# Decoder block on one core: buffers of the mixer's output product and of the cross attention moved to pools of their own

## The chip, the cores and the metric

The kernel runs on one core of a Trainium2 chip (8 cores in two dies; seven of them are idle here). A core has five engines that run their own instruction queues side by side: TensorE (PE, with its weight loads shown as PEld), VectorE (DVE), ScalarE (ACT), GpSimd (POOL) and SyncE (SP, which here only starts transfers). They share an on-chip memory (SBUF, 128 partitions) and 16 DMA engines that move data from and to the main memory. The metric is the device time of one execution in microseconds (us). Differences of under about 0.5% can't be told from no change with this kernel.

## The reference

One decoder layer on `x` (512 tokens x 1024), 256 memory tokens, all in float32:

```
def reference(x, mem, ...):
    x = x + hybrid_mixer(rmsnorm(x, norm_mix_w[l]), ...)           # ends with  mixed @ w_out
    x = x + memory_cross_attention(rmsnorm(x, norm_xa_w[l]), rmsnorm(mem, norm_mem_w[l]), xa_wq, xa_wkv, xa_wo)
    x = x + peer_ffn(rmsnorm(x, norm_ffn_w[l]), ...)               # 8 heads x 16 of 16384 experts per token
    return rmsnorm(x, norm_final_w)

def memory_cross_attention(h, m, wq, wkv, wo):
    q = (h @ wq).reshape(b, s, XA_HEADS, XA_HEAD_DIM)
    k, v = jnp.split(m @ wkv, 2, axis=-1)
    scores = einsum('bshd,bmhd->bhsm', q, k) * XA_HEAD_DIM ** -0.5
    return einsum('bhsm,bmhd->bshd', softmax(scores), v).reshape(b, s, D_MODEL) @ wo
```

`hybrid_mixer` holds two recurrences (gated DeltaNet and mLSTM, four heads each); their outputs, side by side, are `mixed`. `peer_ffn` fetches for every token 128 rows of `u_table` and 128 rows of `v_table`.

## The kernel before

The 512 tokens are four tiles of 128. The work runs in stages: the mixer (with the keys and values of the memory worked in), the mixer's output product, cross attention, the routing of the expert layer, and the expert layer itself, which fetches rows for tiles 0 and 1 with indirect transfers on POOL's queue while tiles 2 and 3 are done densely over the whole tables. A scheduler puts the instructions of each engine in order when the program is built. It also gives every buffer its place: buffers belong to pools, a pool is opened on the left or the right side of the SBUF, and the memory of a closed pool can be given to another one, whose instructions then wait for the instructions that used what lay there.

Three pieces of code meet at the place that changes.

- `mixer` (line 598) opens the pools `mxp` and `mxw` and holds them until its last line. Among the buffers of `mxp` is `hT`, 32 KB a partition. It holds the normed input, transposed and split in a high and a low half, and, under the same name, later `mixed` in the same form (lines 687 to 689).
- The mixer's output product is `residual(..., "wout")` (lines 691 to 692): for tiles 0 and 1, then for tiles 2 and 3, 8 weight blocks of 512 KB each. For a block, SP loads it into one of two buffers `w` (line 246), ACT writes its high half `wh` (236), DVE the low half `wl` (223), and PE does 12 matmuls (271). DVE adds the finished sums to `X` (700). Only when DVE has made the low half may SP load the next but one block.
- `xattn` (704) begins behind it. Its buffers `W0`, `W1`, `W2`, `dh0` and `dh1` are all in the pool `late`, on the right side, over the place of `mxp` and `mxw`. `wr` (the weight row of the norm) is loaded into `W1` by POOL (709, 191). `norm` (724) takes a tile's squares on ACT (197), works out one over the root in 12 small DVE operations (174 to 183), scales on DVE (199), transposes on PE (209) and writes the high half on ACT (211) and the low one on DVE (212) into `dh0` (tiles 0 and 1, called `G0`) or `dh1` (tiles 2 and 3, `G1`). `query` (728) multiplies by `wq`: 8 blocks of 24 matmuls (284) for `G0`, with weights split by ACT (251) into `W2`, their low halves made in turn by POOL (221) and DVE (223).

`ORDER_XA` (line 56) lists the order in which the cross attention and what follows are written: `w2 n0 q008 n1 s0 x0 ...` (weights' buffers, norm of `G0`, its queries in 8 blocks, norm of `G1`, ...).

Of the kernel before, what the change touches and what calls it, by code (L numbers as in the profile page):

```python
# [6 lines left out]
F32 = mybir.dt.float32  # L7
F32R = mybir.dt.float32r
# [8 lines left out]
P = 128  # L17
D = 1024
DB = D // P
# [50 lines left out]
def hymba_kernel(tc, A, out, dbg=None):  # L70
    from contextlib import ExitStack
    with ExitStack() as ctx:
        _body(ctx, tc, A, out, dbg or {})


def _body(ctx, tc, A, out, dbg):
    from contextlib import ExitStack
    nc = tc.nc
    V, SC, PE, G = nc.vector, nc.scalar, nc.tensor, nc.gpsimd

    def pool(name, bufs=1, **kw):
        return ctx.enter_context(tc.tile_pool(name=name, bufs=bufs, **kw))
# [15 lines left out]
    def tap(name, ap):  # L98
        if name in dbg:
            nc.sync.dma_start(dbg[name], ap)  # L100
# [64 lines left out]
    X = {}  # L165
# [36 lines left out]
    def transposed(src, hs, i):  # L202

        ts = slice(i * P, (i + 1) * P)
        for g in range(2):
            ps = psT.tile([P, 4, P], F32, name="tr")
            for b in range(4):
                c = (4 * g + b) * P
                PE.transpose(ps[:, b], src[:, c:c + P], I)
            d = slice(4 * g, 4 * g + 4)  # L210
            SC.activation(hs["h"][:, d, ts], ps, AF.Copy)
            V.tensor_tensor(hs["l"][:, d, ts], ps, hs["h"][:, d, ts], op=OP.subtract)

    def hbuf(ph, n, name="hT"):
        t = ph.tile([P, 2, DB, n * P], F32R, name=name, bufs=1)
        return {"h": t[:, 0], "l": t[:, 1]}
# [9 lines left out]
    low_on, count, spare = [V, G, G], [0], []  # L226
# [31 lines left out]
    def proj(hs, n, w, blocks, evac):  # L258

        for nb in blocks:  # L260
            acc = [psA.tile([P, 512], F32, name="pj") for _ in range(n)]
            for kc in range(4):
                if "f" in hs:
                    pairs = [(hs["f"], unsplit(w[nb, kc], 2))]
                else:
                    pairs = passes((hs["h"], hs["l"]), weights(w[nb, kc]))
                for i in range(n):
                    for z in range(2):
                        d = kc * 2 + z
                        for m, (a, b) in enumerate(pairs):  # L270
                            PE.matmul(acc[i], a[:, d, i * P:(i + 1) * P], b[:, z], start=d == 0 and m == 0,  # L271
                                      stop=d == DB - 1 and m == len(pairs) - 1)
            for i in range(n):
                evac(nb, i, acc[i])
# [53 lines left out]
    def run(steps, n=1000):  # L328
        for _ in range(n):
            if next(steps, steps) is steps:  # L330
                break
# [265 lines left out]

    def mixer(tiles, aside):
        nt = len(tiles)
        with tc.tile_pool(name="mxp", bufs=nt) as ph, tc.tile_pool(name="mxw", bufs=2) as wk:  # L600
            ph = Phase(ph, tiles)
            hs = hbuf(ph, nt)
            mixed = {}
            steps = aside(wk)
            wr = wpool.tile([P, D], F32, name="wh")
# [78 lines left out]
            nc.sync.dma_start(x, A["x"].rearrange("(a p) d -> p a d", p=P))  # L684
            for ti in range(NT):
                X[ti] = x[:, ti]
            hs = hbuf(ph, nt)
            for i, ti in enumerate(tiles):
                transposed(mixed[ti].rearrange("p a b -> p (a b)"), hs, i)
            low_on[:] = [V]  # L690
            for k in range(0, nt, 2):
                residual(tiles[k:k + 2], {z: t[:, :, k * P:(k + 2) * P] for z, t in hs.items()}, "wout")
            for ti in tiles:
                tap(f"x1_{ti}", X[ti])

    def residual(tiles, hs, w):
        def ev(nb, i, ps):
            x = X[tiles[i]]
            c = slice(nb * 512, nb * 512 + 512)
            V.tensor_tensor(x[:, c], ps, x[:, c], op=OP.add)  # L700
        proj(hs, len(tiles), A[w], range(2), ev)
# [365 lines left out]
    def peer_gather(ready, buffer):  # L1067
# [51 lines left out]
        G.dma_start(*close(G0[1]))  # L1119

    mixer(tuple(range(NT)), memory_kv)
    mxs.close()
    late = pool("late", 1, side="right")
# [5 lines left out]
    dh = []  # L1129

    def eight(t):
        return t[:, 0:2].rearrange("p a b -> p (a b)").rearrange("p (a b) -> p a b", a=DB)
    for i in range(2):
        t = late.tile([P, 2, DB, 2 * P], F32R, name=f"dh{i}")
        dh.append({"h": t[:, 0], "l": t[:, 1]})
    pe = ctx.enter_context(ExitStack())
    sct = pe.enter_context(tc.tile_pool(name="sct", bufs=1, side="right"))
# [7 lines left out]
    def row_numbers():  # L1145
        for a in range(K):
            for x, val in enumerate((start[a], start[a] - start[a - 1] if a else 0, a)):
                tc.keep_in_program_order(G.memset(rows_[:, x, a], float(val)))
    pew = pe.enter_context(tc.tile_pool(name="pew", bufs=2, side="right"))

    def opened(g):
        g.open(pe.enter_context(tc.tile_pool(name="pep", bufs=g.nt, side="right")))
        return g
# [15 lines left out]
    def settle(group, ti):  # L1169
        group.finish(ti, slot)  # L1170
        t0 = DENSE.index(ti) * P
        for t in range(t0, t0 + P, TG):
            stages.append(stages.pop(0))
            build(t, bufs, stages[-1], bank4)
            yield

    def ahead(n):
        for _ in range(n):
            ps = psA.tile([P, 512], F32, name="pj")[:, :T]
            times(unsplit(A["pt"][count_a[0]]), second.h, ps)  # L1180
            act_(count_a[0], ps)
            count_a[0] += 1

    def blocks(t):
        return t.rearrange("p a b -> p (a b)").rearrange("p (e t) -> p e t", t=T)
# [9 lines left out]
    for what in ORDER_XA.split():  # L1195
        kind, n = what[0], int(what[1:])
        if kind == "n":
            norm(GS[n])
        elif kind == "q":
            n, x, y = (int(c) for c in what[1:])  # L1200
            query(GS[n], range(x, y))
            if n and y == DB:
                t = late.tile([P, 4, D], F32, name="dh1")
                dh[1] = {"f": eight(t), "room": t}
        elif kind == "s":
            soft_[n] = soft(n)
        elif kind == "x":
            mix(n, *soft_[n])
        elif kind == "o":
            out_(GS[n])  # L1210
        elif kind == "i" and n == 0:
            first = opened(Peer(pew, late, G0))
            rings.extend(lambda nm=nm: wpool.tile([P, D], F32, name=nm) for nm in ("wh", "wl", "wh", "wl"))
            more = late.tile([P, 6, D], F32, name="W2")
            rings.extend(lambda k=k: more[:, k] for k in range(6))
            low_on[:] = [G]
        elif kind == "i":
            second = Peer(pew, late, G1)
            xds.close()
            opened(second)  # L1220
            raws.clear()
            wx = pool("wx", 4)
            rings[:0] = 4 * [lambda: wx.tile([P, D], F32, name="row")]
            raws += [wpool.tile([P, D], F32, name="w") for _ in range(2)] + second.spare
        elif kind == "w":
            raws.clear()
            raws += [wpool.tile([P, D], F32, name="w") for _ in range(2)]
            if n & 1:
                raws += [lo[:, 4 + k] for k in range(2)]
            if n & 2:  # L1230
                raws += [wpool.tile([P, D], F32R, name="wl").bitcast(F32) for k in range(2)]
        elif kind == "f":
            if not n:
                row_numbers()
            first.scores(n)
        elif kind == "u":
            second.scores(n)
        elif kind == "e":
            t = late.tile([P, 6, D], F32, name="W0")
            room.extend(blocks(t[:, k:k + 2]) for k in (0, 2, 4))  # L1240
            room.append(blocks(first.room[:, 0:2]))
        elif kind == "d":
            del rings[-6:-2]
            room.extend(blocks(more[:, k:k + 2]) for k in (0, 2))
        elif kind == "a":
            ahead(n)
        elif kind == "k":
            ready[G0[n]] = first.finish(G0[n], slot)
        elif kind == "p":
            run(gather, n)  # L1250
        else:
            if kind not in flows:
                i, f = {"r": (0, 0), "R": (1, 0), "t": (0, 0), "T": (1, 0), "b": (0, 1), "B": (1, 1)}[kind]
                g = first if kind in "rR" else second
                flows[kind] = settle(g, g.tiles[i]) if f else g.route(g.tiles[i], spot, 2 if kind == "r" else 1)
            run(flows[kind], n)
# [6 lines left out]
    for nm in ("KT", "Vm"):  # L1263
        t = cst.tile([P, 2, D], F32, name=nm)
# [64 lines left out]
```

## Time and profile before

| | |
|---|---|
| three runs | 1854.45, 1844.84, 1854.69 us; median 1854.45 |
| the profiled execution | 1853.35 us, span in the trace 1851.6 us (1.75 us lie around it) |
| busy share of the span | PE 90%, PEld 67%, DVE 69%, ACT 22%, POOL 45% |
| moved | 519 MB, mean 280 GB/s |

A row of the timeline gives start and length in us, the engine, the line of the kernel, the operation, what it writes and reads, and in brackets how long the engine had been idle before and what ended that. `x8` means that eight such instructions were merged in the row. [...] A busy PE is not PE at its peak, and a small part of the matmul records can be missing.

### The profile page before, as it was taken

The page shows a single profiled execution, that of the slowest core. Times are in us where ns is not written, and L with a number is a line of the kernel's source. Part 1 is how long each engine was busy: PE and PEld are TensorE (multiplying, and loading weights), DVE is VectorE, ACT ScalarE, POOL GpSimd, SP SyncE. Part 2 cuts the span into 40 slices and gives each one's busy share as a digit, 9 for nine tenths or more (in the row PEclk, how much of TensorE's full clock was granted, in tenths as well). Part 3 has the DMA queues.
Part 4 walks back from the last instruction along what each step waited for, and adds up shares of the span by engine and source line. Part 5 has one row for each costly group of instructions (what it writes and reads, how often), then busy time and mean ns, then how long its engine had stood idle before and what let it go on. Part 6 is the DMA issues. An engine that isn't in the chain of part 4 may idle for free.

```text
span 1851.6 us, 21460 instructions
## 1 busy us (share of the span) xinstructions
PE 1671.7 (90%) x7468; PEld 1233.1 (67%) x7468; DVE 1269.1 (69%) x2789; ACT 406.2 (22%) x786; POOL 842.2 (45%) x685
## 2 busy tenths in 40 slices
PE   5999999999799976996999879993999999999993
PEld 3878788776598853885888656662666666664441
DVE  6656654665633698999998875557666566566668
ACT  5433532554353131211223110000000000000000
POOL 2121111331123054556354566566666666666663
PEclk9999999999899988998999979997999999999997
DMA  4211211235535477999899999999999999999996
GB/s 139 63 49 43 69 40 46 69 103 193 182 125 171 143 267 276 345 350 347 289 340 395 367 402 410 410 410 409 410 410 410 409 409 410 410 409 409 409 410 253
DMA packets 166508, 519.02 MB, mean 280 GB/s; under 512 B 15744, under 2 KB 44544, under 8 KB 164608
## 3 DMA queue, kind: packets, MB, share of 16 engines
q0 software_dynamic: 76752, 286.82, 39.6%
q1 hardware_dynamic: 60720, 216.15, 31.8%
q10 hardware_dynamic: 28928, 14.68, 2.7%
q8 instruction: 59, 0.97, 0.2%
q14 instruction: 49, 0.40, 0.1%
HBM read 498.71 MB, written 18.87 MB: 280 GB/s over the span
## 4 chain that ended last, share of the span: by engine, by line
DMA 36%; PE 33%; DVE 17%; issue 8%; POOL 4%; ACT 2%; ACTq 1%; SPq 0%; DVEq 0%; POOLq 0%
DMA row<-in_pv,ids 8%; PE pj L313 8%; PE pj L284 7%; PE pj L271 5%; PE acc L445 4%; DMA wh<-in_pv,ids 4%; DMA Vm<-in_pv,ids 3%; DMA W<-gates__132 3%; PE acc L943 3%; DMA W<-in_pv,ids 3%; DMA row<-in_pu,ids 3%; DMA wl<-in_pv,ids 2%; DVE W L1098 2%; DMA wl<-in_pu,ids 2%; DMA KT<-in_pu,ids 2%
## 5 line engine op out<-in xcount | busy, mean ns | idle before, releaser
L998 PE MATMUL o<-ld,W 128*128 128x512 f32 x832 | 371.3, 596 | 4.5 <-DVE W L951 4.5
L313 PE MATMUL pa<-dh,ld 128*128 128x256 f32 x1296 | 295.7, 381 | 35.8 <-ACT dh L970 34.2
L313 PEld LDWEIGHTS pa<-dh,ld 128*128 128x128 f32 x1296 | 247.4, 191 | 104.1 <-issue 39.3
L998 PEld LDWEIGHTS o<-ld,W 128*128 128x128 f32 x832 | 158.9, 191 | 175.9 <-issue 167.5
L221 POOL TENSOR_TENSOR wl<-w,wh 128x1024 fp32r<-128x1024 f32 x32 | 76.9, 2408 | 307.6 <-ACT wh L236 265.8
L313 PE MATMUL pj<-dh,w 128*128 128x256 f32 x640 | 148.0, 387 | 0.2 <-ACT dh L294 0.2
L1071 POOL DMA_INDIRECT W<-in_pu,ids x73 | 95.0, 1302 | 92.1 <-DVE W L1098 53.6
L313 PEld LDWEIGHTS pj<-dh,w 128*128 128x128 f32 x640 | 122.6, 195 | 17.2 <-ACT dh L294 0.7
L1109 DVE SCALAR_TENSOR_TENSOR dh<-row,act,dh 128x1024 f32<-128x1024 f32 x72 | 92.5, 1284 | 57.1 <-DMA row<-in_pv,ids 56.8
L1071 POOL DMA_INDIRECT row<-in_pu,ids x74 | 97.6, 1319 | 60.9 <-issue 19.3
L1071 POOL DMA_INDIRECT row<-in_pv,ids x74 | 99.4, 1343 | 51.3 <-issue 17.4
L970 ACT ACTIVATE W<-pa 128x256 f32<-128x256 f32 x65 | 24.9, 383 | 407.6 <-PE pa L313 397.5
L313 PE MATMUL pj<-dh 128*128 128x256 f32 x496 | 111.7, 379 | 0.0
L271 PE MATMUL pj<-wh,hT 128*128 128x512 f32 x320 | 108.5, 410 | 1.3 <-ACT wh L236 1.3
L284 PE MATMUL pj<-hT,wh 128*128 128x512 f32 x320 | 109.1, 414 | 0.0
L1098 DVE SCALAR_TENSOR_TENSOR row<-row,dh 128x1024 f32<-128x1024 f32 x74 | 88.4, 1222 | 22.5 <-DMA row<-in_pu,ids 22.1
L1098 DVE SCALAR_TENSOR_TENSOR W<-W,dh 128x1024 f32<-128x1024 f32 x73 | 88.5, 1220 | 19.2 <-DMA W<-in_pu,ids 19.2
L313 PEld LDWEIGHTS pj<-dh 128*128 128x128 f32 x496 | 93.5, 191 | 12.2
L236 ACT ACTIVATE wh<-w 128x1024 fp32r<-128x1024 f32 x64 | 67.7, 1058 | 106.8 <-DMA w<-in_wout 27.7
L998 PE MATMUL o<-ld,dh 128*128 128x512 f32 x192 | 85.2, 592 | 0.0
L1071 POOL DMA_INDIRECT wh<-in_pu,ids x40 | 56.6, 1415 | 51.2 <-DVE wh L1098 26.2
L1071 POOL DMA_INDIRECT wl<-in_pu,ids x41 | 54.6, 1332 | 47.8 <-PE pj L313 17.9
(432 smaller groups left out, 3143.5 us busy)
## 6 DMA issues: line engine op xcount, KB each, us to landing
ld<-in_pv SPq DMA_DIRECT2D x128, 512.0 KB, 6.8
ld<-in_pt SPq DMA_DIRECT2D x81, 512.0 KB, 6.9
gates__132<-W ACTq DMA_DIRECT2D x16, 896.0 KB, 16.4
W<-gates__132 POOLq DMA_DIRECT2D x14, 1024.0 KB, 17.4
w<-in_pt SPq DMA_DIRECT2D x24, 512.0 KB, 6.7
dh<-in_pt SPq DMA_DIRECT2D x23, 512.0 KB, 6.7
w<-in_win SPq DMA_DIRECT2D x20, 512.0 KB, 3.6
w<-in_wout SPq DMA_DIRECT2D x16, 512.0 KB, 3.7
```

The costliest lines, as they stand in the source:

```text
L221: G.tensor_tensor(out, a, hi, op=OP.subtract)
L236: SC.activation(hi, wt, AF.Copy)
L271: PE.matmul(acc[i], a[:, d, i * P:(i + 1) * P], b[:, z], start=d == 0 and m == 0, stop=d == DB - 1 and m == len(pairs) - 1)
L284: PE.matmul(acc[:, :n * P], a[:, d], b[:, d], start=d == 0 and m == 0, stop=d == DB - 1 and m == 2)
L313: PE.matmul(ps, w[:, d], h[:, d], start=d == 0, stop=d == DB - 1)
L445: PE.matmul(ps[:, i], l[:, i], r[:, i], start=True, stop=True)
L943: PE.matmul(ps[:, k], oj[:, a, :, k], og[:, g, a, :, k], start=g == 0, stop=g == 1)
L970: SC.activation(place(e), ps, AF.Gelu)
L998: PE.matmul(outs[DENSE[i]][z], place(e)[:, i * P:(i + 1) * P], v[:, z * 512:(z + 1) * 512], start=e == 0, stop=e == NKEY - 1)
L1071: G.indirect_dma_start(out=row, out_offset=None, in_=A[table], in_offset=bass.IndirectOffsetOnAxis(ap=ids[:, s:s + 1], axis=0))
L1098: V.scalar_tensor_tensor(row, row, 1.0, hn, op0=OP.mult, op1=OP.mult, accum_out=act[ti][:, s:s + 1])
L1109: V.scalar_tensor_tensor(hn, row, w, hn, op0=OP.mult, op1=OP.add)
```

## The change

`hT` goes into a pool `mxh` of its own, which the mixer opens first and keeps open over the output product. The rest of the mixer moves into a function `mixed_tiles`, at whose end `mxp` and `mxw` are closed, which is now ahead of the output product. On the other side `dh1` (and what later takes its name) moves from the pool `late` to a pool `later`, opened behind it. In the built program `hT` lies at the bytes 96384 to 129152 of a partition, before and after. `dh1` now lies at 120800 to 137184, over its end; `slot`, `W0`, `W1`, `W2` and `dh0` lie above 137184 and so clear of `hT`, where before `slot` and `W0` lay over its end.

```diff
     def mixer(tiles, aside):
         nt = len(tiles)
+        with tc.tile_pool(name="mxh", bufs=1) as hp:
+            hs = mixed_tiles(tiles, aside, hp)
+
+            low_on[:] = [V]
+            for k in range(0, nt, 2):
+                residual(tiles[k:k + 2], {z: t[:, :, k * P:(k + 2) * P] for z, t in hs.items()}, "wout")
+            for ti in tiles:
+                tap(f"x1_{ti}", X[ti])
+
+    def mixed_tiles(tiles, aside, hp):
+
+        nt = len(tiles)
         with tc.tile_pool(name="mxp", bufs=nt) as ph, tc.tile_pool(name="mxw", bufs=2) as wk:
             ph = Phase(ph, tiles)
-            hs = hbuf(ph, nt)
+            hs = hbuf(hp, nt)
...
-            hs = hbuf(ph, nt)
+            hs = hbuf(hp, nt)
             for i, ti in enumerate(tiles):
                 transposed(mixed[ti].rearrange("p a b -> p (a b)"), hs, i)
-            low_on[:] = [V]
-            for k in range(0, nt, 2):
-                residual(tiles[k:k + 2], {z: t[:, :, k * P:(k + 2) * P] for z, t in hs.items()}, "wout")
-            for ti in tiles:
-                tap(f"x1_{ti}", X[ti])
+            return hs
...
+    lates = late, pool("later", 1, side="right")
     for i in range(2):
-        t = late.tile([P, 2, DB, 2 * P], F32R, name=f"dh{i}")
+        t = lates[i].tile([P, 2, DB, 2 * P], F32R, name=f"dh{i}")
         dh.append({"h": t[:, 0], "l": t[:, 1]})
...
-                t = late.tile([P, 4, D], F32, name="dh1")
+                t = lates[1].tile([P, 4, D], F32, name="dh1")
                 dh[1] = {"f": eight(t), "room": t}
```

Engine by engine the program has the same instructions as before: 5529 on PE, 2245 on DVE, 738 on ACT, 690 on POOL, 421 on SP, in a count that leaves out those that only wait. They stand in another order only between the last third of the output product and the first blocks of the queries of `G0`; ahead of it and behind it the order is the same on each engine, and on POOL throughout. From line 610 on, numbers of lines are 8 to 12 higher in the changed kernel (700 becomes 708).

On PE, before, around the end of the output product (`pj<-wh,hT` are its matmuls, `tr` the transposes of the norm of `G0`, `pj<-dh` with x192 the queries of `G0`):

```order
L271 MATMUL pj<-wl,hT 128x512
L271 MATMUL pj<-wh,hT 128x512 x2
L271 MATMUL pj<-wl,hT 128x512
L271 MATMUL pj<-wh,hT 128x512
L209 MATMUL tr<-UI,W_4066 128x128 x16
L284 MATMUL pj<-dh_4056,W_4065 128x256 x192
```

On PE, now, at the same place:

```order
L271 MATMUL pj<-wl,hT 128x512
L271 MATMUL pj<-wh,hT 128x512 x2
L271 MATMUL pj<-wl,hT 128x512
L271 MATMUL pj<-wh,hT 128x512
L209 MATMUL tr<-UI,W_4073 128x128 x5
L284 MATMUL pj<-dh_4063,W_4072 128x256 x192
```

All 16 transposes stood behind the product; now the last 5 do, and 11 stand in its last third, in groups of 5, 1, 4 and 1.

On ACT, before, from the third weight block of the product on (`wh<-w` is its high half, `W,nss<-x` the squares of a tile, `dh<-tr` a high half of the transposed norm, `W<-w` and `W<-wl` high halves of `wq`):

```order
L236 ACTIVATE wh<-w 128x1024 x14
L197 ACTIVATE W_4066,nss<-x 128x1024 x2
L251 ACTIVATE W_4065<-w 128x1024 x2
L251 ACTIVATE W_4065<-wl 128x1024
L211 ACTIVATE dh_4056<-tr 128x4x128 x2
L197 ACTIVATE W_4066,nss<-x 128x1024
```

On ACT, now:

```order
L236 ACTIVATE wh<-w 128x1024 x7
L197 ACTIVATE W_4073,nss<-x 128x1024
L236 ACTIVATE wh<-w 128x1024
L197 ACTIVATE W_4073,nss<-x 128x1024
L236 ACTIVATE wh<-w 128x1024 x2
L211 ACTIVATE dh_4063<-tr 128x4x128
L236 ACTIVATE wh<-w 128x1024
L211 ACTIVATE dh_4063<-tr 128x4x128
L236 ACTIVATE wh<-w 128x1024 x3
L251 ACTIVATE W_4072<-w 128x1024
L197 ACTIVATE W_4073,nss<-x 128x1024
L211 ACTIVATE dh_4063<-tr 128x4x128 x2
```

Both squares of `G0` and two of its four high halves now stand between weight blocks of the product; the squares of tile 2 stand ahead of the other two high halves.

On DVE, before, from the end of the small operations on that stand behind the product (the rows of 128x1 are those of a norm, `W<-x,nr,W` the scaling of a tile, `W<-w` the low half of the second block of `wq`, `dh<-tr` the low halves of the transposed norm):

```order
L181 TENSOR_TENSOR nt<-nr 128x1
L182 SCALAR_TENSOR_TENSOR nt<-nt,nv 128x1
L199 SCALAR_TENSOR_TENSOR W_4066<-x,nr,W_4067 128x1024
L183 SCALAR_TENSOR_TENSOR nr<-nt,nr 128x1
L223 TENSOR_TENSOR W_4065<-w,W_4065 128x1024
L181 TENSOR_TENSOR nt<-nr 128x1
L182 SCALAR_TENSOR_TENSOR nt<-nt,nv 128x1
L183 SCALAR_TENSOR_TENSOR nr<-nt,nr 128x1
L199 SCALAR_TENSOR_TENSOR W_4066<-x,nr,W_4067 128x1024
L212 TENSOR_TENSOR dh_4056<-tr,dh_4056 128x4x128 x2
```

On DVE, now, behind the last low half of the product (`x<-pj` adds to `X`):

```order
L708 TENSOR_TENSOR x<-pj,x 128x512 x2
L174 TENSOR_SCALAR nv<-nss 128x1
L178 TENSOR_SCALAR nr<-nv 128x1
L179 TENSOR_SCALAR nr<-nr 128x1
L212 TENSOR_TENSOR dh_4063<-tr,dh_4063 128x4x128 x2
L181 TENSOR_TENSOR nt<-nr 128x1
L182 SCALAR_TENSOR_TENSOR nt<-nt,nv 128x1
L183 SCALAR_TENSOR_TENSOR nr<-nt,nr 128x1
L181 TENSOR_TENSOR nt<-nr 128x1
L182 SCALAR_TENSOR_TENSOR nt<-nt,nv 128x1
L183 SCALAR_TENSOR_TENSOR nr<-nt,nr 128x1
L181 TENSOR_TENSOR nt<-nr 128x1
```

The low half `W<-w` stands right behind the last of these rows. Before, the small operations behind the product were those of tiles 0 and 1, and this low half stood behind the first scaling (199) and ahead of the transposes' low halves; now the small operations are those of tile 2, and it stands behind the transposes' low halves.

## Rows read from the trace of the kernel before

**Rows 1.** The page: the span, and the chain that ended last by engine.

```profile
span 1851.6 us, 21460 instructions
DMA 36%; PE 33%; DVE 17%; issue 8%; POOL 4%; ACT 2%; ACTq 1%; SPq 0%; DVEq 0%; POOLq 0%
```

**Rows 2.** The table by stretches: the product's end, the gap, the clock, two other stages.

```profile
461.00:487.40 26.40, 25.37 (x104) 18.54 (x102) 12.99 (x13) 8.28 (x8) 0.00 (x0) 1.00 0.58 177
...
497.20:502.50 5.30, 3.70 (x16) 3.11 (x16) 4.50 (x11) 2.83 (x5) 0.00 (x0) 0.50 0.53 198
...
504.00:505.00 1.00, 1.00 (x7) 1.00 (x6) 0.89 (x10) 0.37 (x2) 0.00 (x0) 0.50 0.00 0
505.00:506.00 1.00, 1.00 (x10) 1.00 (x10) 1.00 (x7) 0.00 (x0) 0.00 (x0) 1.00 0.00 0
...
600.00:650.00 50.00, 50.00 (x255) 44.69 (x254) 33.53 (x205) 8.18 (x18) 2.50 (x9) 1.00 0.44 141
...
1100.00:1200.00 100.00, 100.00 (x354) 66.94 (x353) 59.57 (x87) 5.89 (x16) 62.41 (x44) 1.00 1.03 410
...
130.00:140.00 10.00, 9.57 (x43) 7.00 (x42) 7.57 (x12) 4.21 (x8) 2.16 (x1) 0.82 0.36 104
```

**Rows 3.** PE's timeline from the end of the product to that of the queries.

```profile
487.02 0.40 PE L271 MATMUL pj<-wh,hT 128*128 128x512 f32 x1
497.20 1.94 PE L209 MATMUL tr<-UI,W 128*128 128x128 f32 x8 [9.78 <-issue]
500.74 1.97 PE L209 MATMUL tr<-UI,W 128*128 128x128 f32 x8 [1.60 <-DVE dh L212]
502.54 24.42 PE L284 MATMUL pj<-dh,W 128*128 128x256 f32 x192
```

**Rows 4.** POOL's timeline in the gap.

```profile
487.74 0.74 POOL L191 DMA_DIRECT2D W<-in_nrow  x1 [59.46 <-PE pj L271]
490.68 2.34 POOL L221 TENSOR_TENSOR W<-w,W 128x1024 fp32r<-128x1024 f32 x1 [2.21 <-ACT W L251]
492.99 2.33 POOL L221 TENSOR_TENSOR W<-wl,W 128x1024 fp32r<-128x1024 f32 x1
```

**Rows 5.** ACT's timeline in the gap.

```profile
487.46 1.06 ACT L197 ACTIVATE W<-x 128x1024 f32<-128x1024 f32 x1 [4.18 <-PE pj L271]
488.42 0.19 ACT L197 ACTIVATION_READ_ACCUMULATOR W<-x 128x1 f32 x1
...
498.33 0.60 ACT L211 ACTIVATE dh<-tr 128x512 fp32r<-128x512 f32 x1 [5.84 <-PE tr L209]
```

**Rows 6.** DVE's timeline, in the product and in the gap.

```profile
468.17 1.23 DVE L223 TENSOR_TENSOR wl<-w,wh 128x1024 fp32r<-128x1024 f32 x1 [2.62 <-ACT wh L236]
...
487.46 0.69 DVE L700 TENSOR_TENSOR x<-pj,x 128x512 f32<-128x512 f32 x1 [0.71 <-PE pj L271]
...
490.56 0.23 DVE L182 SCALAR_TENSOR_TENSOR nt<-nt,nv 128x1 f32<-128x1 f32 x2
490.76 2.35 DVE L183 SCALAR_TENSOR_TENSOR nr<-nt,nr 128x1 f32<-128x1 f32 x2
493.14 2.20 DVE L181 TENSOR_TENSOR nt<-nr 128x1 f32<-128x1 f32 x1
...
495.82 1.28 DVE L199 SCALAR_TENSOR_TENSOR W<-x,nr,W 128x1024 f32<-128x1024 f32 x1 [0.28 <-DMA W<-in_nrow]
...
497.09 1.22 DVE L223 TENSOR_TENSOR W<-w,W 128x1024 fp32r<-128x1024 f32 x1
```

**Rows 7.** What SP's queue waited for, 434 to 530 us; the product's weight loads.

```profile
SPq L246 <- DVE wl L223: 34.7, 15, 2.8
...
w<-in_wout SPq DMA_DIRECT2D x14, 512.0 KB, 3.7
```

**Rows 8.** DVE's and POOL's timeline at a later place, behind the queries.

```profile
528.02 2.36 POOL L221 TENSOR_TENSOR W<-wl,W 128x1024 fp32r<-128x1024 f32 x1 [3.35 <-ACT W L251]
528.73 1.29 DVE L212 TENSOR_TENSOR dh<-tr,dh 128x512 fp32r<-128x512 f32 x2 [2.36 <-ACT dh L211]
```

## The prediction

> **What bounds the kernel now.** I read the page's chain of waits first [rows 1]: the end is set by transfers for 36% of the span and by PE for 33%, so the kernel has stages with different limits. The table by stretches tells them apart [rows 2]: at 600 to 650 us PE is busy for all of the 50 us; at 1100 to 1200 the DMA engines are at 1.03 and move 410 GB/s. The change touches neither of them but the seam at 487 us, so PE's timeline was next [rows 3]. The last matmul of the output product ends at 487.42 (487.02 and 0.40). Then PE has no work for 9.78 us, does 8 transposes, waits another 1.60, does 8 more, and begins the queries of tiles 0 and 1 at 502.54; these end at 526.96. From the end of the product to that of the queries that is 39.5 us.
>
> Why PE stands idle is to be seen on the other engines. POOL's load of the norm's weight row has waited 59.46 us for PE, and is let go only when the product is over [rows 4]. ACT takes the first squares at 487.46, 4.18 us after its last work, again on PE's release [rows 5], though tile 0 was complete long before. So it is not data but memory that they wait for: everything the cross attention writes lies over what the product still reads. The scaling on DVE then starts at 495.82, when the row has landed [rows 6]. [...]
>
> **The change part by part.**
>
> *The wait of tiles 0 and 1 goes.* With `hT` alone in its pool, the row's load may start behind the last transposes of `mixed`, ahead of most of the product, and the squares of tiles 0 and 1 as soon as their sums are complete, in the middle of the product. The order shows that the scheduler took this up: 11 of 16 transposes stand inside the product. What is late next is the rest of the chain below.
>
> *The product itself gets slower.* Its weight loop is tight: SP's loads wait for the low half on DVE (34.7 us in 15 waits), and a load takes 3.7 us [rows 7], so every us by which DVE or ACT makes a block later is one for PE. Put into the last third are, on DVE, 24 small operations (two in 0.20 us when two chains alternate: 490.56 to 490.76; so 2.4 us, or twice that when they don't), 2 scalings of 1.28 [rows 6] and 2 low halves of 0.65 (1.29 for two) [rows 8]: 6.3 to 8.7 us. On ACT 2 squares of 1.06 with 0.19 for the sum, and 2 high halves of 0.60 [rows 5]: 3.7 us. There is room for it: in these 26.4 us DVE is busy 12.99 and ACT 8.28 [rows 2]. Bounds: 0 us if all falls in the room, 12.4 if all lands on the loop (a gain is excluded: nothing leaves the loop). Step by step, ahead of the low half at 468.17 DVE was idle for 2.62 [rows 6]; now 18 small operations and a scaling stand there, 1.8 + 1.28 = 3.1, so it comes 0.5 late. Later ACT's second high half must wait for transposes ahead of a weight block, 0.4 more. The row's 512 KB now travel beside the product's loads, about 0.4. I take 1.3: the product ends at about 488.7. The 11 transposes fall in PE's waits of the product (25.37 us busy in 26.40) [rows 2].
>
> *From the product to the queries.* Call its end T. Tile 2's last matmul comes some 1.5 us ahead of T (6 of the stretch's 96 matmuls, which took 25.37 [rows 2]), so ACT takes its squares from about T - 0.65 (behind 0.69 for the sum [rows 6]) to T + 0.6; then come the two high halves that are left, to T + 1.15 and T + 1.7. DVE adds tile 3's sums, does three small operations, and the first low half is done at T + 2.0. The queries' matmuls can run from there. Bounds: 1.2 (a high and a low half right behind T) to 5.3 (what the 8 transposes and waits between 497.20 and 502.54 take now [rows 3]).
>
> *The queries.* 24.42 us now [rows 3], of which 2.46 (to 505.0) at half the clock [rows 2]; without that 23.2. I count the clock as full since PE rests for some 1.5 us only. Bounds 23.2 to 24.4.
>
> *A new wait.* Block 0's low half is made on POOL in time. Block 1's is DVE's, and stands behind seven small operations of tile 2. In the trace such small operations stick while POOL makes a low half: two took 2.35 us beside POOL's 490.68 to 493.02, the next 2.20 beside its second [rows 4, 6]. Low halves from PSUM don't (1.29 for two beside POOL's at 528.02) [rows 8]. Now POOL starts block 2's low half at T + 2.8, when ACT has its high half, and holds it until T + 5.1; DVE comes to the seven at T + 2.65. So they are through at T + 6.1, and block 1's low half (1.22) at T + 7.3. PE wants it at T + 5.1, one block (2.9 us) and two matmuls after its start: 2.2 us of waiting. Bounds: 0, and 4.7 if a second low half of POOL (2.33) gets in between.
>
> [...]
>
> *Behind the queries* every engine's order is as before. Nothing there waits for a time, only for data and for buffers, so all of it should come earlier by the same amount, the DMA-bound stage too.
>
> **Sum.** Instead of 39.5: 1.3 + 2.0 + 23.2 + 2.2 = 28.7 us. That is 10.8 less; the profiled execution's 1853.35 becomes 1842.6. It lies 1.1 below the median of the runs, 1854.45, so the median should come to 1843.7. Ends of the sum: 0 + 1.2 + 23.2 + 0 = 24.4, a gain of 15.1 (1839.3), and 12.4 + 5.3 + 24.4 + 4.7 = 46.8, a loss of 7.3 (1861.8).
>
> **The rivals.**
>
> *The inserted work lands on the weight loop.* Price up to 12.4 us instead of 1.3, so no gain, 1855. For it: DVE and ACT work strictly in order, and the loop has no slack of its own. Against: both engines are idle for half of the stretch. Half of it on the loop (6.2) gives a gain of 5.9, 1848.5.
>
> *The DMA-bound stage takes the gain back.* If transfers set the end from 1100 us on whatever comes before, the time stays 1854. For it: 410 GB/s without a break [rows 2]. Against: the stage's fetches start from indices that the queries lead to, in the same order, so the stage as a whole moves.
>
> *The clock falls, and the kernel gets slower.* Place: the last third of the product, where PE now has more and shorter waits. Such a fall can come with little idling: at 130 to 140 us PE is busy for 9.57 of 10 us and the clock is 0.82 [rows 2]. [...] It decides from 21.6 us at half the clock on (half of them lost). Against: the product has run at 1.00 with such waits, and the long rest goes. [...]
>
> *More than forecast.* No wait on block 1 and no stretch: 1839. The three runs lie 10 us apart, so a median can also fall lower, to about 1835.
>
> **How the numbers follow.** Forecast, with its own range of 1839.5 to 1847: 0.60. Work on the loop (1847 to 1854): 0.17. Taken back (1854): 0.10. Clock (1868): 0.07. More (1835 to 1839.5): 0.06. What this kernel's runs can tell from no change is 0.5%, 9.3 us, so faster means below 1845.2, slower above 1863.7. Of the forecast's 0.60 I put 0.50 below that line. Faster 0.50 + 0.06 = 0.56, same 0.10 + 0.17 + 0.10 = 0.37, slower 0.07. The range of 8 in 10 runs from 1835 to 1854: it leaves out the slower case, and some at both ends.
>
> **What would show it.** PE's wait of 9.78 us ahead of the transposes is gone, and 11 of them stand before the product's last matmul. Squares on ACT begin at about 462, and POOL's row load waits for the transposes of `mixed`, not for the product. The product ends 0 to 3 us later than 487.4; the queries start about 2 us behind and end near 516, with one wait of about 2 us for DVE's low half in their second block. The clock is 1.00 from 461 to 520. All later marks (the first gather, the last store) come about 11 us earlier. I am wrong if the product stretches by more than 5 us, if PE waits in several blocks of the queries, or if the marks at 650 and 1100 us don't both move by what the queries' end moves.

## The result and the profile after

The changed kernel takes 1840.22 us, median of 15 runs (1835.18 to 1847.36); the kernel before, on the same chips, 1850.37, median of 15 (1844.83 to 1859.73). The ratio is 0.9944, its 95% interval 0.9929 to 0.9960: 10.2 us less, where 10.8 were forecast. That is 0.56%, just past the 0.5% that this kernel's runs can tell from no change, and the interval excludes a ratio of 1. The profiled execution took 1840.22 us, its span is 1838.1 where [rows 1] had 1851.6; these two profiles are called the first pair below. The first lines of the page after:

```profile
span 1838.1 us, 21460 instructions
DMA 35%; PE 34%; DVE 18%; issue 6%; POOL 4%; ACT 2%; ACTq 1%; SPq 0%; DVEq 0%; POOLq 0%
```

The shares of the chain hardly change, since the seam is only about 2% of the span (39.5 of 1851.6 us before, 27.3 of 1838.1 now); where the time went can only be read at the seam itself. PE's timeline at the seam (start, busy time, the operation, and in brackets the wait ahead of it and what ended it) answers to [rows 3]:

```profile
487.08 0.39 PE L271 MATMUL pj<-wh,hT 128*128 128x512 f32 x1
487.31 0.71 PE L209 MATMUL tr<-UI,W 128*128 128x128 f32 x5
488.75 0.39 PE L284 MATMUL pj<-dh,W 128*128 128x256 f32 x1 [0.74 <-ACT dh L211]
489.48 3.25 PE L284 MATMUL pj<-dh,W 128*128 128x256 f32 x25 [0.34 <-DVE dh L212]
494.61 20.18 PE L284 MATMUL pj<-dh,W 128*128 128x256 f32 x166 [1.88 <-DVE W L223]
514.63 1.04 PE L209 MATMUL tr<-UI,W 128*128 128x128 f32 x8
```

The product ends at 487.47, as before (487.42). The wait of 9.78 us is gone; five transposes are left behind the product, the other eleven stand inside it. The queries' matmuls run from 489.48 and end at 514.79 (a next matmul starts some 0.16 us ahead of the modelled end of the last), 12.17 us earlier than in [rows 3]. From the end of the product to that of the queries it is 27.3 us instead of 39.5. One wait is new, 1.88 us in the second block, as 26 matmuls stand ahead of it and a block has 24.

The same stretches on ACT, POOL and DVE, for [rows 4 to 6]. ACT:

```profile
461.11 1.06 ACT L197 ACTIVATE W<-x 128x1024 f32<-128x1024 f32 x1 [0.15 <-DVE x L708]
...
487.07 1.06 ACT L197 ACTIVATE W<-x 128x1024 f32<-128x1024 f32 x1 [0.41 <-DVE x L708]
...
488.12 1.06 ACT L211 ACTIVATE dh<-tr 128x512 fp32r<-128x512 f32 x2
489.08 1.06 ACT L251 ACTIVATE W<-wl 128x1024 fp32r<-128x1024 f32 x1
490.03 1.05 ACT L251 ACTIVATE W<-w 128x1024 fp32r<-128x1024 f32 x1
```

POOL:

```profile
437.86 0.74 POOL L191 DMA_DIRECT2D W<-in_nrow  x1 [12.86 <-PE tr L209]
486.75 2.37 POOL L221 TENSOR_TENSOR W<-w,W 128x1024 fp32r<-128x1024 f32 x1 [48.14 <-ACT W L251]
490.21 2.41 POOL L221 TENSOR_TENSOR W<-wl,W 128x1024 fp32r<-128x1024 f32 x1 [1.10 <-ACT W L251]
```

DVE:

```profile
466.50 1.28 DVE L199 SCALAR_TENSOR_TENSOR W<-x,nr,W 128x1024 f32<-128x1024 f32 x1
467.70 1.22 DVE L223 TENSOR_TENSOR wl<-w,wh 128x1024 fp32r<-128x1024 f32 x1
...
490.32 2.32 DVE L183 SCALAR_TENSOR_TENSOR nr<-nt,nr 128x1 f32<-128x1 f32 x1
492.67 0.16 DVE L181 TENSOR_TENSOR nt<-nr 128x1 f32<-128x1 f32 x1
...
493.33 1.23 DVE L223 TENSOR_TENSOR W<-w,W 128x1024 fp32r<-128x1024 f32 x1
```

The first square of tile 0 starts at 461.11, released by DVE's sum and no longer by PE; the row's load goes out at 437.86 behind the transposes of `mixed`. The cause of the new wait is to be read across the last two views: POOL makes the low half of block 2 from 490.21 to 492.62 (`W<-wl`; the high half of block 2 comes ahead of block 1's on ACT), a small operation of DVE that needs 0.16 us elsewhere lasts from 490.32 to 492.64, and block 1's low half (493.33) is queued behind it.

The table by stretches, for [rows 2] and with the same columns: the stretch in us from the span's start, its length, the busy time (and instructions) of PE, PE's weight loads, DVE, ACT and POOL, the clock that TensorE was granted as a share of its full speed, the busy share of the DMA engines, GB/s. All records of the clock in the traces of before and after are at 1.00 or 0.50, so a value between is a mean of the two.

```profile
461.00:487.40 26.40, 25.65 (x112) 19.33 (x111) 18.38 (x41) 11.98 (x15) 0.65 (x1) 1.00 0.54 169
487.40:491.00 3.60, 2.52 (x19) 2.08 (x18) 3.30 (x9) 3.60 (x7) 2.50 (x2) 1.00 0.90 299
491.00:494.00 3.00, 1.74 (x15) 1.53 (x13) 2.86 (x6) 2.44 (x5) 1.62 (x1) 1.00 0.76 306
494.00:505.00 11.00, 10.39 (x86) 10.39 (x87) 9.29 (x19) 3.99 (x6) 3.09 (x2) 1.00 0.70 233
...
1100.00:1200.00 100.00, 100.00 (x347) 65.49 (x346) 58.27 (x88) 5.75 (x15) 62.15 (x45) 1.00 1.03 410
```

In the last third of the product DVE is busy for 18.38 us instead of 12.99 and ACT for 11.98 instead of 8.28, in the same 26.40. The clock is at 1.00 in the last third of the product and all through the seam, where before it was at 0.50 from 491.3 to 505.0 us. At 1100 us the DMA engines move 410 GB/s as before.

Behind the seam both traces hold the same instructions in the same order, so one can set each against its twin. The first matmuls of the next stage (`acc<-subk`), before:

```profile
658.64 0.61 PE L821 MATMUL acc<-subk,pqT 128*128 128x128 f32 x4
```

and after:

```profile
646.47 0.61 PE L829 MATMUL acc<-subk,pqT 128*128 128x128 f32 x4
```

12.17 us earlier, to the hundredth what the queries' end moved. Further on the difference wanders: PE's matmuls are 15.8 us earlier at 700, 17.0 at 1100, 11.2 from 1320 to the last one; 240 MB have been moved 13.0 us earlier (1139.7 instead of 1152.7), and this 13.0 stays until 480 MB at 1726. The span is 13.5 shorter. What of that is the change, and what only these two executions, the experiments had to tell.

### The profile page after: what moved, and what is told of

It reads as the page before. It is cut to its first block, busy times and chain, and to the rows that moved or that the text cites. A ratio compares the mean times of both kernels' runs of the same rounds, so it can differ in the third digit from the quotient of the medians.

```text
span 1838.1 us, 21460 instructions
## 1 busy us (share of the span) xinstructions
PE 1670.5 (91%) x7468; PEld 1231.9 (67%) x7468; DVE 1268.3 (69%) x2789; ACT 405.9 (22%) x786; POOL 839.3 (46%) x685
## 4 chain that ended last, share of the span: by engine, by line
DMA 35%; PE 34%; DVE 18%; issue 6%; POOL 4%; ACT 2%; ACTq 1%; SPq 0%; DVEq 0%; POOLq 0%
PE pj L313 8%; PE pj L284 7%; DMA row<-in_pv,ids 6%; PE pj L271 6%; DMA Vm<-in_pv,ids 5%; DMA wh<-in_pv,ids 4%; PE acc L445 4%; PE acc L951 3%; DMA wl<-in_pv,ids 3%; DMA wh<-in_pu,ids 3%; DMA KT<-in_pv,ids 3%; DMA W<-gates__132 2%; DVE W L1106 2%; DMA W<-in_pv,ids 2%; DVE row L1106 2%
## 5 line engine op out<-in xcount | busy, mean ns | idle before, releaser
L978 ACT ACTIVATE W<-pa 128x256 f32<-128x256 f32 x65 | 24.9, 383 | 408.1 <-PE pa L313 352.9
L313 PEld LDWEIGHTS pj<-dh 128*128 128x128 f32 x496 | 93.5, 191 | 12.2
```

Of the source, the lines that this page charges most:

```text
L313: PE.matmul(ps, w[:, d], h[:, d], start=d == 0, stop=d == DB - 1)
L978: SC.activation(place(e), ps, AF.Gelu)
```

## The experiments

The kernels ran in three groups of four ("call" in the expectations); those of a group share a chip and the runs of the kernel before. All of them compute the whole reference. A single run scatters by some 3 us (standard deviation of the change's 35 runs), so by an estimate from that the difference of two medians of 6 to 12 runs has a standard error of about 2 us, and a step of 4 us between them can be chance. The seam is read from the profiles, where it repeats to 0.3 us but for one step, told below.

| Kernel (group) | median us, runs | less the change's in the group | product to queries' end, us | last 96 matmuls of the product, us |
|---|---|---|---|---|
| before (1, 2, 3) | 1853.28, 1850.49, 1851.34 | +12.4, +7.9, +12.0 | 39.54 | 24.91 |
| ht_only (1) | 1853.49, 12 | +12.6 | 39.62 | 25.16 |
| later_only (1) | 1853.12, 12 | +12.2 | 39.28 | 25.34 |
| the change: first pair | 1840.22, 15 | | 27.32 | 25.88 |
| again (1) | 1840.91, 6 | | 28.83 | 25.93 |
| again2 (2) | 1842.62, 8 | | 28.82 | 25.91 |
| again3 (3) | 1839.35, 6 | | 27.32 | 25.38 |
| low_v (1) | 1839.35, 10 | -1.6 | 25.29 | 25.49 |
| low_v_b (3) | 1837.64, 6 | -1.7 | 25.28 | 25.76 |
| low_g (2) | 1843.31, 9 | +0.7 | 29.20 | 25.62 |
| scale3 (2) | 1836.83, 6 | -5.8 | 27.34 | 26.38 |
| scale3_b (3) | 1839.18, 9 | -0.2 | 27.34 | 26.57 |
| shift (2) | 1848.88, 12 | +6.3 | 35.96 | 25.92 |
| shift8 (3) | 1858.64, 12 | +19.3 | 48.23 | 25.48 |

**Both halves of the change, one at a time.** Either of them alone leaves every engine's order as it was before.

```
ht_only:     lates = late, late
later_only:  hs = hbuf(ph, nt), and the product inside the pool mxp, as before; lates as in the change
```

Expected of ht_only:

> Only hT is put in a pool of its own; both dh buffers stay in the pool late. Theory (a pool is waited for as a whole, and late lies over hT): W0 and the slots still lie over hT, so the row load and the squares wait for the product's last matmul, PE's wait of about 9.8 us is back, product to queries takes 39 to 40 us, ratio 0.999 to 1.001. Rival (only what lies over hT itself waits): W0 waits but dh0 and the row's buffer W1 don't, the row load comes early, and about 2 us of the gain are seen, ratio 0.998 to 0.9995.

Expected of later_only:

> Only dh1 is put in a pool of its own; hT stays in the pool mxp, which is closed behind the product. Now W0, W1, W2 and dh0 all lie at addresses that hT does not touch, only mixed does, and mixed has been read long before. Theory (the pool as a whole is waited for): nothing is gained, product to queries takes 39 to 40 us, ratio 0.999 to 1.001. Rival (addresses alone decide): the whole gain is here already, 27 to 28 us, ratio 0.994 to 0.996.

Neither gains: ratio 0.9994 (0.9976 to 1.0011) and 1.0001 (0.9983 to 1.0019). PE's timeline of ht_only:

```profile
498.08 1.94 PE L209 MATMUL tr<-UI,W 128*128 128x128 f32 x8 [9.81 <-issue]
501.61 1.97 PE L209 MATMUL tr<-UI,W 128*128 128x128 f32 x8 [1.59 <-DVE dh L212]
503.42 24.46 PE L284 MATMUL pj<-dh,W 128*128 128x256 f32 x192
```

PE's and POOL's timeline of later_only:

```profile
496.39 1.94 PE L209 MATMUL tr<-UI,W 128*128 128x128 f32 x8 [9.43 <-issue]
```

```profile
487.29 0.74 POOL L191 DMA_DIRECT2D W<-in_nrow  x1 [62.57 <-PE pj L271]
```

In later_only the row's buffer lies where it does in the change, at other addresses than `hT`, and its load still waits 62.57 us for the product's last matmul: the pool is waited for as a whole. In ht_only the row's buffer doesn't lie over `hT` either, but its pool does, in `W0`. So the rivals of both runs fall; the change works only when both pools are apart.

**The change again,** without an edit.

> The changed kernel once more, unchanged, for a second profile and for the comparison with the other runs. Theory (the seam gives the gain, the rest is a shift): PE from the end of the output product to the end of the queries of tiles 0 and 1 takes 27.3 us again, within 0.5, the median ratio is 0.994 to 0.996, and the steps that the first pair of profiles shows elsewhere (10 us lost or won at 646 to 690, 5.7 us at 1260 to 1317, a pause of the DMA engines at 1074 to 1084) come at other places or in other sizes, since they would be scatter of the transfers. Rival (those steps belong to the change): they stand at the same places, with the same sizes within 1 us.

> The changed kernel a third time, beside the three others of this call, and for a third profile. In the second profile the granted clock fell to 0.50 for some 3 us right behind PE's wait of 1.88 us in the queries, in the first it did not. Theory (the wait leaves the clock on an edge): product to queries takes either 27.3 us (no fall) or about 28.8 us (fall), nothing between. Rival (the second profile was disturbed by something else): 27.3 us, and any fall of the clock stands elsewhere.

> The changed kernel beside the three others of this call. Theory (scatter of the transfers): its median stands 9 to 12 us below the kernel before. Product to queries is 27.3 us or, with a fall of the clock, 28.8. Rival: none, it is the measure for the three others.

The expectation of again failed in two points: its seam is 28.83 instead of 27.3, and its ratio to the kernel before is 0.9927 (0.9899 to 0.9955), below the 0.994 that was written down. Over the four profiles only two values appear for the seam, 27.3 and 28.8, each twice. Where it is 28.8 the last 166 matmuls of the queries take longer (again, PE's timeline):

```profile
493.95 21.68 PE L284 MATMUL pj<-dh,W 128*128 128x256 f32 x166 [1.88 <-DVE W L223]
```

and the table by stretches shows why (again):

```profile
490.00:494.00 4.00, 2.12 (x19) 1.91 (x17) 3.86 (x9) 2.78 (x5) 1.95 (x1) 1.00 0.65 246
494.00:497.00 3.00, 3.00 (x15) 3.00 (x16) 2.93 (x8) 0.00 (x0) 0.00 (x0) 0.55 0.61 205
497.00:498.00 1.00, 1.00 (x8) 1.00 (x7) 0.83 (x6) 0.00 (x0) 0.00 (x0) 0.63 1.00 406
498.00:516.00 18.00, 18.00 (x152) 18.00 (x152) 5.32 (x7) 8.45 (x13) 7.39 (x3) 1.00 0.64 204
```

Right behind the wait the clock is at 0.55 on average for 3 us and at 0.63 for one more, which costs 21.68 - 20.18 = 1.5 us. In again2 it falls at the same place, behind a wait of 1.87 that ends at 492.53 (table by stretches):

```profile
492.00:493.00 1.00, 0.47 (x3) 0.47 (x4) 1.00 (x6) 0.00 (x0) 0.00 (x0) 0.86 0.04 16
493.00:496.00 3.00, 3.00 (x16) 3.00 (x16) 2.86 (x7) 0.00 (x0) 0.00 (x0) 0.50 0.82 262
```

If only the levels 1.00 and 0.50 occur, as in the traces of before and after, 0.86 means 0.28 us at 0.50, so by this estimate it falls at 492.72. So the two values of again2's theory appear, with nothing between, and its rival falls. The wandering behind the seam, on the other hand, is scatter: against the first pair's before, ht_only and later_only, which run the same instructions, have 240 MB moved 3.5 us later and 2.1 us earlier, and of the 3.3 us by which the change's first profile was ahead at 430 us, 2.6 came at 140, long before the edit. At 440 to 447 it lost 2.7 again, behind a weight load of 9.58 us, and ht_only and later_only lose 3.0 and 2.9 there too: in all three the clock is at 0.94 on average from 434 to 461, where the first pair's before has 1.00. Between profiles of the change 240 MB come at 1133.1 to 1139.7.

The two steps on PE that the expectation of again names come at the same places there and within 1 us of the first pair's sizes: from 646 to 700 us a further 3.1 us are won against before (first pair: -12.2 to -15.8, so 3.6), and up to 1320 us 5.0 are lost (first pair: 5.8). By the letter that is the rival's sign. But ht_only and later_only, in the old order, win 3.8 and 3.8 at the first place and lose 3.1 and 5.2 at the second: both steps are mostly long or short waits in the one profile of before that all of them are compared with, and not the change's. again3 has the first one (4.1) and nothing of the second. The third mark, the pause of the DMA engines at 1074 to 1084 us, is there in another size: 266 GB/s in the first profile, 368 in again.

**The new wait.**

```
  query(GS[n], ...)   preceded by   low_on[:] = [V] if n == 0 else [V, G]     (low_v)
                                    low_on[:] = [G] if n == 0 else [V, G]     (low_g)
```

> The changed kernel with all eight low halves of the first queries on DVE (before: every other one on POOL). Theory (block 1's low half comes late since two-input operations of DVE stick beside POOL's low half): no small operation there lasts over 0.3 us, PE's wait of 1.88 us for block 1's low half is gone, the restart behind the product is at most 0.5 us later, product to queries takes 25.3 to 26.2 us, and the end comes 1.2 to 2 us earlier than with the change alone. Rival (DVE's queue is simply too full behind the product): the wait stays or grows by up to 1.2 us, the end is 0 to 1.2 us later.

> The low halves of the first queries on DVE, once more. Theory (no wait in the queries, so no fall of the clock behind it): product to queries 25.3 us again, clock 1.00 there, median 1.5 to 4 us below the change's of this call. Rival (what is won there is lost in the scatter of the gathers): within 1.5 us of it.

> The changed kernel with all eight low halves of the first queries on POOL. Theory (the wait of 1.88 us is block 1's low half on DVE, stuck beside POOL's; POOL needs 2.4 us a block, PE 2.9): the wait is gone, three or more small operations of DVE last 2.2 to 2.4 us, product to queries takes 25.2 to 26 us, the clock stays at 1.00 there, and the end comes 1.2 to 2.5 us earlier than with the change alone. [...]

low_v, PE's timeline:

```profile
488.78 0.38 PE L284 MATMUL pj<-dh,W 128*128 128x256 f32 x1 [0.74 <-ACT dh L211]
489.51 23.28 PE L284 MATMUL pj<-dh,W 128*128 128x256 f32 x191 [0.34 <-DVE dh L212]
```

and DVE's:

```profile
490.20 1.22 DVE L223 TENSOR_TENSOR W<-wl,W 128x1024 fp32r<-128x1024 f32 x1
491.34 1.22 DVE L223 TENSOR_TENSOR W<-w,W 128x1024 fp32r<-128x1024 f32 x1
...
493.43 0.16 DVE L181 TENSOR_TENSOR nt<-nr 128x1 f32<-128x1 f32 x1
```

191 matmuls without a wait, the small operations at 0.16, 25.29 us for the seam, and 25.28 in the second run; the clock stays at 1.00 in both. The medians are 1.6 and 1.7 us below the change's: the size expected, at the edge of what they can tell (all runs pooled, 16 against 35: -2.0, interval -4.0 to about 0). It has the shortest seam here; its ratio to the kernel before is 0.9934 (0.9911 to 0.9956) and 0.9926 (0.9901 to 0.9952). The run alone doesn't tell the stuck operation from DVE's order, since block 1's low half now also stands ahead of most of tile 2's small operations. The rows of the change do: the one operation that sticks there takes 2.32 us instead of 0.16, which is 2.16 more and so covers the wait of 1.88.

low_g failed. POOL's timeline:

```profile
484.43 2.42 POOL L221 TENSOR_TENSOR W<-wl,W 128x1024 fp32r<-128x1024 f32 x1 [1.01 <-ACT W L251]
486.79 2.36 POOL L221 TENSOR_TENSOR W<-w,W 128x1024 fp32r<-128x1024 f32 x1
```

and PE's:

```profile
489.21 21.67 PE L284 MATMUL pj<-dh,W 128*128 128x256 f32 x166 [2.26 <-POOL W L221]
```

POOL works in the order in which ACT makes the high halves, block 2 ahead of block 1. Block 1's low half now stands behind a whole operation of POOL and comes 7.5 us after the product (481.68), later than the 7.1 on DVE. The wait is 2.26, the clock falls behind it (0.50 from 490 to 492), and the seam is 29.20. I had left that order out. Small operations stuck as expected (2.33, 2.27, 2.29, 2.29, 2.40 us), off the path.

**Room in the product.**

```
  for _ in range(1 + more):       # more = 2 for tiles 0 and 1
      V.scalar_tensor_tensor(xn, x, r, w, op0=OP.mult, op1=OP.mult)
```

> The changed kernel with the scaling of tiles 0 and 1 done three times instead of once (four more DVE operations of 1.28 us, 5.1 us, in the last third of the output product, same result). Theory (DVE has room there: 18.4 us busy of 26.4): the last 96 matmuls of the product take 0.3 to 2.0 us longer than the change's 25.9, PE's later steps are as they were, the end is 0.3 to 2.5 us later than the change's. Rival (what is inserted lands on the weight loop): 4 to 5.1 us longer, the end 4 to 5.5 us later.

> The scaling of tiles 0 and 1 three times, once more: in the first run its product took 0.5 us longer, as the theory has it, but its median came 5.8 us below the change's of that call, which neither theory has. Theory (scatter between chips and runs; the four operations are free): its median is 2 us below to 2.5 us above the change's of this call. Rival (the extra work helps, by a shift of the product against the transfers or by a clock that does not fall behind the product): again 3 us or more below it, and in the profile no fall of the clock at 490 to 500 us.

Of 5.1 us more on DVE the last 96 matmuls show 26.38 and 26.57, against 25.78 as the mean of the change's four profiles: 0.7 us, so they fall in the room. The table by stretches of scale3, over the same part:

```profile
458.00:485.00 27.00, 25.55 (x112) 19.27 (x111) 23.00 (x45) 12.16 (x15) 1.34 (x1) 1.00 0.53 170
```

DVE at 23.00 of 27, and still room. The first median, 5.8 us below the change's, was in neither theory; the second, beside the change on another chip, is 0.2 below. Its seam is 27.34 both times, as in the change without a fall of the clock, so nothing in the profiles answers to the 5.8; it is best taken as scatter, and as a warning on what six runs are worth.

**Does the shift reach the end?**

```
  for d in range(DB if nb in again else 0):     # again = (5, 6, 7) in shift, all 8 in shift8
      for m, (a, b) in enumerate(passes(wt, hT)):
          PE.matmul(acc..., start=d == 0 and m == 0, stop=...)     # the same block once more
```

> The changed kernel with the matmuls of the last three blocks of the first queries done twice (72 more matmuls of 0.122 us, 8.8 us of PE, same result). Theory (behind the queries everything is a shift, the stage bound by transfers too): the queries end 8.8 us later, transfers reach 300 MB 6 to 10 us later than in the change's profiles (1286 us), the end is 7.5 to 9.5 us later than the change's median of this call, 1848 to 1851 us. Rival (the stage bound by transfers takes it back): the end moves by less than 2 us, 1840 to 1843.

> The changed kernel with the matmuls of all eight blocks of the first queries done twice (192 more of 0.120 us, 23.0 us of PE, same result; waits inside the queries of 1.9 us may vanish beside it). Theory (all that follows is a shift): the end comes 20 to 23.5 us later than the change's median of this call. Rival (the stages bound by transfers take back a part, as the 6.3 us of 8.6 in the run with three blocks might say): 12 to 18 us later.

In shift the seam is 35.96 us, 7.9 more than the change's mean of 28.07; 240 MB come at 1149.3 (1133.1 to 1139.7 in the change; the product too ends 2.9 to 6.6 us later in this profile); the median is 6.3 more than the change's. In shift8 the wait of 1.88 us is hidden and no fall of the clock follows (1.00 from 486 to 515), so the seam is 48.23, 20.2 more, not 23; the median is 19.3 more. Both fall short of the ranges that I wrote down (7.5 and 20), since these left out that the change's seam is sometimes 28.8 and that shift8 takes the wait away. Against what the seam really grew by, 6.3 of 7.9 and 19.3 of 20.2 arrive. The profiles show it more closely. From the end of the queries to the moment at which 240 MB have been moved it is 622.1 to 624.9 us in the change's four profiles, 623.0 in shift and 622.4 in shift8, and from there to the end of the span 698.4 to 699.6 us in every profile of this case. That the stages bound by transfers take the shift back is excluded; that they take a tenth of it is not.

## Why the prediction was right

*The wait goes.* As put: the cause was memory, not data. The two halves alone show more than the prediction said: what is waited for is the pool, not the address.

*The product gets slower by 1.3.* Too much by more than half: the last 96 matmuls take 24.91, 25.16 and 25.34 us in the three profiles of the old order and 25.88, 25.93, 25.91 and 25.38 in the change's, 25.14 and 25.78 on average, so 0.6. One profile of each could not have told; in the first pair the product even ended at the same time, since its last 96 matmuls began 0.93 us earlier. What the row's load, which now runs beside the first half of the product, costs there (0.4 in the forecast) can't be told: the first 96 matmuls take 28.3 to 31.0 us in the old order and 28.6 to 31.5 in the change's four profiles. The room was larger than counted, as scale3 shows.

*Restart 2.0.* 487.47 to 489.48: 2.0, with the high halves of `dh` at T + 0.65 to 1.7 (T is the end of the product) as worked out, behind tile 2's square.

*Queries 23.2 at full clock.* 514.79 - 489.48 - 1.88 = 23.4, and 24.9 in half of the profiles. Here the reason was incomplete: I let the clock be full because PE rests for some 1.5 us only, and did not ask the same of the wait that the next step adds: with a wait of 1.87 to 1.90 us at this place the clock fell in two profiles of seven, with 2.26 in the only one, without the wait in none of three (low_v, low_v_b, shift8). Each of the three falls stands right behind the wait; three profiles without it are few to show that it never falls there. The same kernel has a seam of 27.3 us in two profiles and of 28.8 in two; what tells them apart no run here shows.

*The new wait 2.2.* 1.88, by the path that was written down: the seven through at T + 5.9 (6.1 predicted), the low half done at T + 7.1 (7.3). The stuck operation (2.32 us instead of 0.16) ends with POOL's (492.64 and 492.62), and where POOL makes no low half (low_v) these operations last 0.14 to 0.16 us and the wait is gone.

*The sum.* 28.7 predicted; 0.6 + 27.3 = 27.9 or 0.6 + 28.8 = 29.4 measured, a gain of 11.6 or 10.1. Over all groups and the first pair the change's 35 runs have a median of 1841.0, the kernel before's 84 one of 1851.5: 10.5 us (9.4 to 12.3, by drawing the runs anew). The errors of two terms (0.7 too much on the product, 0.7 too little for the clock on average) cancel, and that is luck. The time itself came 3.5 us below the 1843.7 that was forecast, mostly since the three runs of before that it started from stood 4.1 above the median of all fifteen.

*Behind the queries all shifts.* Right at 646 us to the hundredth; at 1100 the first pair shows 17.0 on PE and 13.0 on the transfers, which by the letter of the prediction would have spoken against it. That test was too sharp for one pair of profiles: the gathers move such marks by 3 us either way in kernels with the same instructions. The runs shift and shift8 carry the point instead, with the time from the queries' end to 240 MB, which keeps within a few us whatever the seam takes.

*The rivals.* Work on the loop: refuted, 0.6 us and 0.7 of 5.1. Taken back: refuted as a whole, though not for a tenth of it. The clock: not in the last third of the product, where it stayed at 1.00, but in the queries, at 1.5 us. The 1868 among the chances counts 24.3 us for it, each of the product's 25.37 busy us taken for two at half the clock; no run shows that. In the trace of before the queries' matmuls start 0.213 us apart at 0.50 (503.9 to 504.9 us) and 0.120 apart at 1.00, a factor of 1.78, so by an estimate from these the 25.37 would have become 45 and the price 19. More than forecast: its mechanism (no wait on block 1) is low_v, a further 2.0 us of the seam. Its price was added up wrongly: without the 2.2 and the 1.3, 1843.7 becomes 1840.2 and not 1839.

## What to carry to other kernels

When every engine starts a stage only behind the last instruction of the one before it, look at what memory the new stage is given: a pool is waited for as a whole, so a single long-lived tensor in it, or a single buffer over it, holds back all the rest, and both sides must be split. Work that then moves into a loop with a tight chain was nearly free here, where the engines have idle time between the loop's steps (0.6 us of PE for 9.1 us of work on DVE and ACT). A short wait that is left over is worth more than its length when TensorE's clock can fall behind it (1.88 us and, in two profiles of seven, another 1.5), and moving the late operation to the idle engine helps only if that engine's queue doesn't put something ahead of it.

## What the runs showed of the hardware beyond that

The clock's fall was not the same in every execution of one kernel: the same instructions with the same wait (1.87 to 1.88 us) lost 1.5 us to it in again and again2 and nothing in the first pair and again3. What decides is open here.

Small operations of DVE stuck beside POOL's operations of 128x1024 (two inputs, 2.3 to 2.4 us) as follows. In the traces of before and after, those of 128x1 with two inputs from SBUF (`TENSOR_TENSOR` and `SCALAR_TENSOR_TENSOR`, 0.14 to 0.16 us elsewhere) that started behind POOL's start and over 0.1 us ahead of its end lasted until 0.01 to 0.02 us behind that end, all eight: 2.20 to 2.32 us where they started up to 0.2 us behind POOL (490.76 and 493.14 before, 490.32 and 498.74 after), 1.32 where 1.06 behind (23.42 before, 22.39 after), 0.86 and 0.87 where 1.56 behind (583.01 and 570.84). In low_g five took 2.27 to 2.40 us. Those that started 0.02 to 0.12 us ahead of POOL took 0.15 to 0.16. Operations of 128x1 with one input (`TENSOR_SCALAR`) took 0.14 to 0.16 us beside POOL's as elsewhere, and those with one of the two inputs from PSUM 0.21 to 0.22 us (line 585, five times in each trace; 0.20 to 0.22 elsewhere). That the number of inputs decides is not shown: in before a `TENSOR_SCALAR` of 128x4 took 1.78 us (323.29) and one of 128x8 2.37 (208.81) beside POOL's, instead of 0.17.
